# A list scheduler that counts loads of ScalarE's function tables, with another table of due times

## The chip, the cores and the metric

One Trainium2 chip; the kernel runs on one of its cores. The metric is the device time of one execution in microseconds (us). Engines are called as in the profile: PE (TensorE matmul, PEld its weight loads), DVE (VectorE), ACT (ScalarE), POOL (GpSimd), SP (the engine that only issues DMAs).

## What is computed

One layer of a hybrid block on 512 positions of width 1024, in float32:

```python
h = rmsnorm(x) ; proj = h @ w_in                 # gb, gc, v | u, ug | q | three gates
y_a = (gb * conv3(gc * v)) @ w_a_out             # short gated convolution
y_b = silu(layernorm(conv31(u * sigmoid(ug)))) @ w_b_out
y_c = attention(q, rmsnorm(mem) @ w_kv) @ w_att_out    # 4 heads, 256 memory tokens
m = sigmoid(g0) * y_a + sigmoid(g1) * y_b + sigmoid(g2) * y_c
x = x + m @ w_o
up = conv3(rmsnorm(x) @ w_up) ; x = x + (silu(gate half) * up half) @ w_down   # width 2816
return rmsnorm(x)
```

## The kernel before

**Arithmetic.** Each float32 operand of a product is split in two fp32r parts, high and low, and three products are added: high by high, low by high, high by low. ACT makes the high part by a cast (weights "wh", line 481; activations "fh", line 1357), DVE the low part by a subtraction ("wl", line 485; "fl", line 1361). A weight tile thus goes from its DMA over ACT and DVE to PE.

**Quads.** The large products are computed by a Strassen-like scheme: seven products for a 2 by 2 block, a *quad* (names glu, q, gate, cv, bb, mq, up). The sums of weights that the scheme needs are made by DMAs of POOL that add to what has landed ("s3", "s5", "s6", "s7", line 606). The products' banks are read out by ACT ("r1", "r5", "r6", "r4") and DVE ("r2", "r7", "r3"): r6 reads the bank of product 6 (line 701), which product 7 overwrites; r4 is the last read of ACT (line 709).

**Stages in order of time.** Keys and values of the memory (line 915 and the products K and V); the projection quads; between them the attention (exponentials, line 1068) and the 31 taps of branch B ("tp" on ACT, line 1224, two per job; sums on DVE, line 1231); from about 438 us LayerNorm statistics, the gates' sigmoids (line 1481, two or four per row), the swish of branch B (line 1322), whose casts (line 1357) feed the last projection quads "mq" (branch B's output product, 510 to 552 us); the product by w_o (lines 432 to 434), in seven parts a, b, f, c, d, e, g, with additions to x on DVE (line 1719); the second RMSNorm: square (line 1726), root (1732), reciprocal (1736), scaling (1737), transpose on PE (1745); then the up quads, the FFN's convolution and silu gate, the down products and the last norm.

**The order of work.** PE's order is written by hand. All other instructions are *jobs* of a list scheduler (`Jobs.run`), which replays the program with estimated costs and issues, step by step, the job that can start first; of several, the one that is due first. A job's due time comes from `latest_starts`: the planned start of the product that needs it, less the costs on the way, plus a number for its kind from the table LATER. A kind in AHEAD also isn't started earlier than so many us before it is due. The order found is frozen, so that it is the order of each engine's queue. These two lines of `run` choose:

```python
rank = (start, due[key])
if best is None or rank < best[0]:
```

The scheduler of before knows no function tables: where a job on ACT uses a function that isn't in the table loaded last, the compiler puts a load (ACT_TABLE_LOAD) ahead of it. Sigmoid, silu (swish), exponential and square root lie in different tables; copies, casts and squares need none.

Of the kernel before, what the change touches and what calls it, by code (L numbers as in the profile page):

```python
# [61 lines left out]
SHARE = 0.39  # L62
SEEN = {"PE": 0.2, "ACT": 0.14, "DVE": 0.12}
# [7 lines left out]
    "ACT fh y t4": 45, "ACT pth": -72, "ACT r1 mq": -5, "ACT r4 cv": 36, "ACT r4 gate": 12.12,  # L71
    "ACT r5 gate": 28.56, "ACT sigmoid": 32.54, "ACT tp 1": -18.64, "ACT tp 2": 21.22,
# [5 lines left out]
    "DVE tap 2": -72, "DVE tap 3": 173, "DVE top": 49, "DVE vl": 125, "DVE weigh": 125,  # L78
# [9 lines left out]
    "ACT fh y t7": 5, "ACT r4 gate": 5, "ACT r5 gate": 40, "ACT sigmoid": 80, "ACT tp 1": 150,  # L88
# [25 lines left out]
class Jobs:  # L114
# [109 lines left out]
    def run(self, log=None):  # L224
# [4 lines left out]
        for key, j in self.jobs.items():  # L229
            waits[key] = len(set(j[3]))  # L230
            if j[0] == "PE":
                pe.append(key)
            elif not waits[key]:
                ready.setdefault(j[0], {})[key] = 0.0
            for name in j[6]:
                self.left[name][0] += 1
        free = {e: 0.0 for e in ["PE"] + sorted({j[0] for j in self.jobs.values()} - {"PE"})}
        pe.reverse()
        n = len(self.jobs)
        while n:  # L240
            best = None
            for e in free:
# [74 lines left out]
def hybrid_block_kernel(  # L317
# [19 lines left out]
    nc = tc.nc  # L337
# [340 lines left out]
    def quad_reads(q, first, second, ring, after=(), all_but_4=False):  # L678
# [16 lines left out]
        job(("r1", q), "ACT", actv(512), read1, [(q, 1)] + list(after),  # L695
# [3 lines left out]
        job(("r5", q), "ACT", actv(512), read5, [(q, 5)] + list(after),  # L699
            take=[(second, ring)], use=[bank("b")])  # L700
        job(("r6", q), "ACT", actv(512), lambda: nc.scalar.copy(f()[:, :, hi_t], view("a")),
# [7 lines left out]
        job(("r4", q), "ACT", actv(512), lambda: nc.scalar.activation(  # L709
# [1071 lines left out]
    for t in range(NT):  # L1781
# [8 lines left out]
        for i in range(2):  # L1790
            bank, r = ("bank", "tr", t, i), t // 2
            if (i, r) != (0, 1):
                job(("rh", t, i), "ACT", actv(512), lambda t=t, i=i: row_high(t, i), [("tr", t)],
# [5 lines left out]
            job(("rb", t, i), "ACT", actv(512), lambda t=t, i=i: row_block(t, i), [("tr", t)],  # L1799
# [508 lines left out]
```

## Time and profile before

| what | value |
|---|---|
| median of 3 runs (range) | 930.26 us (929.43 to 931.14) |
| the profiled execution | 929.14 us |
| its span, first to last instruction | 927.4 us |
| mean granted TensorE clock | 0.997 |
| busy: PE, DVE, ACT, POOL | 98%, 91%, 74%, 15% of the span |
| loads of function tables on ACT in the order | 13 |

How to read it: a row of the timeline has the start, the duration, the engine, the line of the program, the operation, what it writes and reads by the program's names, and in brackets how long the engine sat idle before it and what ended that. A row with x2 stands for two instructions in a row. The table by stretches has the busy time and the count of each engine in each stretch. All of it is of one execution.

### The profile page before, as it was taken

How to read it: one execution, taken by the hardware profiler on the slowest of the kernel's cores; microseconds unless marked ns; L12 is line 12 of the kernel's file. 1: busy time of each engine (PE TensorE's matmuls, PEld its weight loads, DVE VectorE, ACT ScalarE, POOL GpSimd, SP SyncE). 2: the span in 40 equal slices, each digit the busy share in tenths (PEclk: the TensorE clock that was granted, in tenths of full speed). 3: DMA queues.
4: the chain of work that ended last, by engine and by line, in shares of the span. 5: the costliest groups of instructions: out<-in, count | busy, mean ns of one | idle time of the engine just before them, and what ended most of it. 6: DMA issues, size and time to landing. Idle time of an engine off the chain costs nothing.

```text
span 927.4 us, 17128 instructions
## 1 busy us (share of the span) xinstructions
PE 912.5 (98%) x6821; PEld 861.6 (93%) x6821; DVE 847.8 (91%) x973; ACT 685.8 (74%) x935; POOL 137.0 (15%) x165
## 2 busy tenths in 40 slices
PE   9999999999999999999999999999999999999996
PEld 8999999999989999999899897799999999988885
DVE  6998999999979999999886999897999889999986
ACT  7567988889978876878766982786766667765665
POOL 0121111101011111110111111111221111002300
PEclk9999999999999999999999999999999999999998
DMA  9999678845588888888858899899999885689952
GB/s 355 389 243 220 143 183 199 189 114 114 155 181 232 199 191 203 215 198 207 198 130 219 195 250 327 213 231 305 275 248 235 193 168 125 176 310 310 252 110 91
DMA packets 55952, 196.91 MB, mean 212 GB/s; under 512 B 6336, under 2 KB 6464, under 8 KB 55872
## 3 DMA queue, kind: packets, MB, share of 16 engines
q0 software_dynamic: 22608, 81.54, 48.6%
q1 hardware_dynamic: 32544, 113.23, 33.6%
q8 instruction: 53, 0.87, 0.4%
q10 hardware_dynamic: 720, 1.06, 0.3%
q14 instruction: 27, 0.22, 0.1%
HBM read 191.60 MB, written 4.19 MB: 211 GB/s over the span
## 4 chain that ended last, share of the span: by engine, by line
PE 88%; ACT 5%; DVE 3%; DMA 2%; issue 1%; SPq 0%; ACTq 0%; DVEq 0%
PE bank L658 57%; PE bank L432 6%; PE bank L434 6%; PE bank L433 6%; PE bank L1456 3%; PE bank L1457 3%; PE bank L1458 3%; PE bank L915 2%; ACT whi L481 1%; DVE wlo L485 1%; DMA wf<-in_w_up 1%; PE bank L1690 1%; DMA wf<-in_w_v 1%; ACT acc L1322 1%; PE ss L788 0%
## 5 line engine op out<-in xcount | busy, mean ns | idle before, releaser
L481 ACT CAST whi<-wf 128x1024 fp32r<-128x1024 f32 x202 | 210.7, 1045 | 90.0 <-PE bank L658 36.5
L485 DVE TENSOR_TENSOR wlo<-wf,whi 128x1024 fp32r<-128x1024 f32 (+1 forms) x196 | 236.3, 1213 | 21.7 <-ACT whi L481 21.5
L1224 ACT ACTIVATE tp<-u,pk 128x510 f32<-128x510 f32 (+22 forms) x184 | 119.2, 706 | 4.5 <-DVE acc L1231 2.1
L1231 DVE TENSOR_TENSOR acc<-acc,tp 128x988 f32<-128x988 f32 (+22 forms) x92 | 109.3, 1189 | 8.8 <-ACT tp L1224 7.3
L606 POOL DMA_DIRECT2D wf<-in_w_in x48 | 42.4, 899 | 233.4 <-DVE wlo L485 165.5
L658 PE MATMUL bank<-fb10h,whi 128*128 128x256 f32 x248 | 69.0, 278 | 1.6 <-ACT g L709 1.2
L658 PE MATMUL bank<-ft4h,whi 128*128 128x256 f32 (+1 forms) x249 | 68.7, 276 | 0.9 <-DVE y L438 0.9
L658 PE MATMUL bank<-fb10l,whi 128*128 128x256 f32 x248 | 68.6, 277 | 0.6 <-DVE fb10l L1361 0.6
L658 PE MATMUL bank<-ft6h,whi 128*128 128x256 f32 (+1 forms) x250 | 68.8, 277 | 0.2 <-ACT gt L686 0.2
L658 PE MATMUL bank<-ft5l,whi 128*128 128x256 f32 x248 | 68.8, 277 | 0.0
L658 PE MATMUL bank<-ft6l,whi 128*128 128x256 f32 x248 | 68.7, 277 | 0.0
L658 PE MATMUL bank<-ft5h,whi 128*128 128x256 f32 (+1 forms) x251 | 68.7, 276 | 0.0
L658 PE MATMUL bank<-fb11h,wlo 128*128 128x256 f32 x248 | 68.6, 277 | 0.1
L658 PE MATMUL bank<-fb11h,whi 128*128 128x256 f32 x248 | 68.7, 277 | 0.0
L658 PE MATMUL bank<-fb00h,whi 128*128 128x256 f32 (+1 forms) x250 | 68.7, 276 | 0.0
L658 PE MATMUL bank<-ft6h,wlo 128*128 128x256 f32 x248 | 68.6, 277 | 0.0
L658 PE MATMUL bank<-fb00l,whi 128*128 128x256 f32 x248 | 68.6, 277 | 0.0
L658 PE MATMUL bank<-ft4l,whi 128*128 128x256 f32 x248 | 68.6, 276 | 0.0
L658 PE MATMUL bank<-ft5h,wlo 128*128 128x256 f32 x248 | 68.5, 276 | 0.0
L658 PE MATMUL bank<-ft7h,whi 128*128 128x256 f32 x248 | 68.5, 276 | 0.0
L658 PE MATMUL bank<-ft7l,whi 128*128 128x256 f32 x248 | 68.5, 276 | 0.0
L658 PE MATMUL bank<-ft7h,wlo 128*128 128x256 f32 x248 | 68.5, 276 | 0.0
(406 smaller groups left out, 3167.7 us busy)
## 6 DMA issues: line engine op xcount, KB each, us to landing
wf<-in_w_in SPq DMA_DIRECT2D x52, 512.0 KB, 5.4
wf<-in_w_in POOLq DMA_DIRECT2D x48, 512.0 KB, 6.1
wf<-in_w_up POOLq DMA_DIRECT2D x31, 512.0 KB, 7.3
wf<-in_w_up SPq DMA_DIRECT2D x29, 512.0 KB, 7.9
wf<-in_w_down SPq DMA_DIRECT2D x15, 512.0 KB, 4.4
wf<-in_w_att_out SPq DMA_DIRECT2D x8, 512.0 KB, 3.6
wf<-in_w_a_out SPq DMA_DIRECT2D x8, 512.0 KB, 3.6
wf<-in_w_b_out SPq DMA_DIRECT2D x8, 512.0 KB, 6.2
```

Of the source, the lines that this page charges most:

```text
L432: nc.tensor.matmul(ps, s_hi, w_hi, start=start, stop=False, skip_group_check=again)
L433: nc.tensor.matmul(ps, s_hi, w_lo, start=False, stop=False, skip_group_check=again)
L434: nc.tensor.matmul(ps, s_lo, w_hi, start=False, stop=stop, skip_group_check=again)
L481: nc.scalar.copy(parts[0], src())
L485: nc.vector.tensor_tensor(lo, src(), hi.bitcast(F32), op=ALU.subtract)
L606: nc.gpsimd.dma_start(out=tiles[key], in_=block(w, col[c], k), accum_op=ALU.add)
L658: nc.tensor.matmul(ps[:, c, part], w[:, k, at], a[k][:, part], start=first and n == 0 and part.start == 0, stop=k == 3 and n == 2, skip_gr ...
L1224: nc.scalar.activation(two(("tp", p, s))[:, j, s:], two(("u", p))[:, j, : SEQ - s], AF.Copy, scale=weight(j),)
L1231: nc.vector.tensor_tensor(a, a, two(("tp", p, s))[:, :, s:], op=ALU.add)
L1456: nc.tensor.matmul(ps, w_hi[:, i, at], hi, start=first, stop=False)
L1457: nc.tensor.matmul(ps, w_hi[:, i, at], lo, start=False, stop=False)
L1458: nc.tensor.matmul(ps, w_lo[:, i, at], hi, start=False, stop=last)
```

## The change

No instruction of arithmetic and no DMA is added or removed, and PE's order stays. Four things change in the planning.

1. The scheduler keeps the table that is loaded. A job that needs another one, and isn't due within 3 us, is ranked as if it started 1.28 us later; a job that changes the table costs 1.28 us more in the plan.
2. The planned cost of ACT's reads of a bank in the quads and behind the second norm falls from (n + 224)/1200 - 0.08 to (n + 68)/1200 us, for 512 columns from 0.53 to 0.48.
3. The planned costs of a quad's product and of a whole w_o product fall by under 1.2%.
4. The tables LATER and AHEAD are replaced by longer ones, with an entry for most kinds of jobs and shifts of up to 1500 us.

```diff
+TABLES = {
+    "ACT sg": "sigmoid", "ACT sigmoid": "sigmoid", "ACT swish": "silu", "ACT silu": "silu",
+    "ACT exp": "exp", "ACT m root": "sqrt", "ACT x root": "sqrt", "ACT v root": "sqrt",
+    "ACT xroot": "sqrt", "ACT rt": "sqrt",
+}
+TABLE_LOAD, TABLE_WAIT = 1.28, 3.0
...
 LATER = {
-    "ACT fh y t4": 45, "ACT pth": -72, "ACT r1 mq": -5, "ACT r4 cv": 36, "ACT r4 gate": 12.12,
+    "ACT c3": -619, "ACT exp": -81, "ACT fh h b00": -432.7, "ACT fh h b10": -180,
...
+        table = None
...
-                        rank = (start, due[key])
+                        late = TABLES.get(self.kind(key), table) != table
+                        late = late and due[key] + lag - start > TABLE_WAIT
+                        rank = (start + TABLE_LOAD if late else start, due[key])
                         if best is None or rank < best[0]:
-                            best = (rank, e, key, got)
+                            best = (rank, e, key, got, start)
...
-            (start, _), e, key, got = best
+            _, e, key, got, start = best
             _, cost, fn, after, latency, _, names = self.jobs[key]
+            if TABLES.get(self.kind(key), table) != table:
+                table, cost = TABLES[self.kind(key)], cost + TABLE_LOAD
...
+    def from_bank(n):
+        return (n + 68) / 1200.0
...
-    MM, MM_HALF, MM_QUAD = 0.2268, 0.12, 0.1142
-    MM_WHOLE = 0.87
+    MM, MM_HALF, MM_QUAD = 0.2268, 0.12, 0.1135
+    MM_WHOLE = 0.86
...
-        job(("r6", q), "ACT", actv(512), lambda: nc.scalar.copy(f()[:, :, hi_t], view("a")),
+        job(("r6", q), "ACT", from_bank(512), lambda: nc.scalar.copy(f()[:, :, hi_t], view("a")),
```

About 460 of 738 jobs on ACT stand at another place than before (by up to 35), 612 of 899 on DVE (by up to 72), 110 of 220 on SP (by up to 6) and 59 of 157 on POOL (by up to 6). Line numbers of the changed kernel are higher by 102 behind the tables. ACT has 11 loads of tables: between the root of the LayerNorm (row 416 in both) and the end of the mq quads there were five, for sigmoid, silu, sigmoid, silu, sigmoid, and are three, sigmoid, silu, sigmoid. One pair of sigmoids moves ahead of the LayerNorm's root, another behind the fifth load. At the read r6 of the last cv quad, the largest difference of that part, eleven jobs of taps and a weight cast now stand ahead of it that stood behind, and two casts and one bias product behind it that stood ahead.

Three places, in rows of the order (line, operation, tiles with their numbers, shape). First ACT in the mq stage, where the swish of the last channel blocks (acc_3230 and acc_3978; acc_3197 and acc_3917 in the changed kernel) is cast for the product with fb10. Before:

```order
L481 CAST whi_6112<-wf_5878 128x1024
L1481 ACT_TABLE_LOAD
L1481 ACTIVATE g_5783<-g_5783,pk 128x512 x2
L686 COPY y_6145<-bank_6082 128x2x256
L1357 CAST ft6h_6149<-acc_1093 128x512
L481 CAST whi_6153<-wf_5923 128x1024
L1357 CAST ft4h_6156<-acc_3230 128x512
L1322 ACT_TABLE_LOAD
L1322 ACTIVATE acc_3978<-acc_3978,pk 128x512 x2
L686 COPY y_6191<-bank_6120 128x2x256
L1357 CAST fb10h_6078<-acc_3978 128x512
```

And the changed kernel:

```order
L583 CAST whi_6103<-wf_5958 128x1024
L1459 CAST fb10h_6109<-acc_3197 128x512
L1459 CAST fb11h_6113<-acc_3197 128x512
L1459 CAST ft7h_6116<-acc_1093 128x512
L1424 ACTIVATE acc_3917<-acc_3917,pk 128x512 x2
L788 COPY y_6150<-bank_6078 128x2x256
L1459 CAST fb10h_6109<-acc_3917 128x512
L583 CAST whi_6154<-wf_5888 128x1024
```

The two loads and the pair of sigmoids between the last two swish jobs are gone; the sigmoids of g_5783 stand some 20 rows further down, behind those of g_5924.

Second, ACT behind w_o, the norm of the first two row tiles of x. Before:

```order
L481 CAST whi_6799<-wo_6664 128x1024
L1726 ACTIVATE xnorm_6812,cols<-x_833_6520 128x1024
L1726 ACTIVATE xnorm_6815,cols<-x_841_6564 128x1024
L1732 ACT_TABLE_LOAD
L1732 ACTIVATE cols<-cols,eps 128x1 x2
L481 CAST whi_6833<-wf_6690 128x1024
```

And the changed kernel:

```order
L583 CAST whi_6786<-wo_6695 128x1024
L1828 ACTIVATE xnorm_6800,cols<-x_839_6560 128x1024
L1834 ACT_TABLE_LOAD
L1834 ACTIVATE cols<-cols,eps 128x1
L583 CAST whi_6818<-wo_6634 128x1024
L1828 ACTIVATE xnorm_6831,cols<-x_842_6599 128x1024
L583 CAST whi_6840<-wf_6778 128x1024
```

The first root stands ahead of the second square; the second root comes behind both. On DVE the low part of whi_6818 takes the place of the second scaling, between the first scaling and the next two additions to x.

Third, SP at the start of the program, where mem are half tiles of the memory and wf weights. Before:

```order
L850 DMA wf_98<-in_w_v 128x512 x2
L511 DMA wf_119<-in_w_v 128x1024
L741 DMA mem_99<-in_mem_t 128x512 x2
L511 DMA wf_151<-in_w_kv 128x1024
L511 DMA wf_168<-in_w_kv 128x1024
```

And the changed kernel:

```order
L952 DMA wf_98<-in_w_v 128x512 x2
L843 DMA mem_99<-in_mem_t 128x512 x2
L613 DMA wf_128<-in_w_v 128x1024
L613 DMA wf_151<-in_w_kv 128x1024
L613 DMA wf_172<-in_w_kv 128x1024
```

The weight V(0,1) is loaded behind the two half tiles instead of ahead of them, and ACT's casts of it and of the half tiles change places in the same way.

More of the change, by code (lines that the diff above doesn't have):

```diff
@@ new lines @@
+    "ACT sr": -334, "ACT swish": 252, "ACT tap 1": -214.4, "ACT tap 2": -191, "ACT tap 3": -547.5,
[8 rows of a table added]
+    "ACT wn wo 0": -774.4, "ACT x root": 121, "ACT xroot": -5.5, "ACT xsq": -18, "ACT xsquare": 15,
[8 rows of a table added]
+    "DVE low": 39.7, "DVE m scale": -418, "DVE mgl a": 159, "DVE mgl b": 325.5, "DVE mgl d": 11,
+    "DVE mgl e": 647.4, "DVE mgl g": -351, "DVE ml": 15, "DVE ms c": -142, "DVE ms d": -3.5,
+    "DVE ms e": 328, "DVE msum": -143, "DVE mu fold": -89, "DVE mu low": -614, "DVE mu sum": -395,
+    "DVE ol": -34, "DVE pn": -193, "DVE ptl": -147, "DVE ql": -1183.6, "DVE r2 bb": -176.3,
[5 rows of a table added]
@@ L85 @@
+    "DVE rd f": -4, "DVE rd g": 51.4, "DVE sc": -297.1, "DVE sum": -988.2, "DVE tap 1": -30,
+    "DVE tap 2": 25.4, "DVE tap 3": 51.2, "DVE top": -7.9, "DVE tot1": -8, "DVE tot2": -44,
+    "DVE um": -1259, "DVE var fold": 4.7, "DVE var sum": -23.3, "DVE vl": 737, "DVE weigh": 547,
[18 rows of a table added]
+    "POOL s7 up": -142, "POOL wadd e": -277, "POOL wadd x": 2.1, "POOL wadd y": -65,
[6 rows of a table added]
 }
 AHEAD = {
-    "ACT fh y t7": 5, "ACT r4 gate": 5, "ACT r5 gate": 40, "ACT sigmoid": 80, "ACT tp 1": 150,
[4 rows of a table removed]
+    "ACT fh h b00": 80, "ACT fh h b11": 150, "ACT fh h t4": 40, "ACT fh h t6": 40,
@@ new lines @@
+    "ACT rt": 10, "ACT sq": 150, "ACT tap 1": 10, "ACT tap 2": 20, "ACT tap 3": 150,
[4 rows of a table added]
+    "ACT wn merge 0": 5, "ACT xroot": 40, "ACT xsquare": 150, "ACT zh c": 150, "ACT zh g": 5,
+    "DVE CV": 80, "DVE c3": 80, "DVE centre": 150, "DVE ends": 150, "DVE fl h b00": 150,
[5 rows of a table added]
+    "DVE ol": 150, "DVE pn": 20, "DVE ptl": 40, "DVE ql": 5, "DVE r2 glu": 20, "DVE r2 q": 5,
+    "DVE r2 up": 40, "DVE r3 gate": 150, "DVE r3 glu": 80, "DVE r3 q": 10, "DVE r7 bb": 20,
+    "DVE r7 gate": 20, "DVE r7 glu": 2, "DVE r7 mq": 10, "DVE r7 up": 40, "DVE rd a": 40,
@@ L93 @@
+    "DVE rd c": 2, "DVE rd d": 150, "DVE rd f": 40, "DVE sum": 150, "DVE top": 5, "DVE tot1": 20,
[5 rows of a table added]
+    "DVE xnorm": 150, "DVE xsum": 5, "DVE y t4": 10, "DVE y t5": 150, "DVE y t6": 10,
[5 rows of a table added]
+    "POOL wadd x": 150, "POOL wadd y": 80, "POOL wl merge 0": 10, "POOL wl merge 2": 20,
[4 rows of a table added]
 }
@@ L693, in add @@
             nc.vector.tensor_tensor(t, t, b, op=ALU.add)
-        job(("r1", q), "ACT", actv(512), read1, [(q, 1)] + list(after),
+        job(("r1", q), "ACT", from_bank(512), read1, [(q, 1)] + list(after),
             take=[(first, ring)], use=[bank("a")])
@@ L698, in quad_reads @@
             [(q, 2), ("r1", q)], use=[bank("c"), first])
[L699 removed]
+        job(("r5", q), "ACT", from_bank(512), read5, [(q, 5)] + list(after),
             take=[(second, ring)], use=[bank("b")])
[L701 removed]
+        job(("r6", q), "ACT", from_bank(512), lambda: nc.scalar.copy(f()[:, :, hi_t], view("a")),
             [(q, 6), ("r1", q)], use=[bank("a"), first])
@@ L708, in quad_reads @@
             return
-        job(("r4", q), "ACT", actv(512), lambda: nc.scalar.activation(
+        job(("r4", q), "ACT", from_bank(512), lambda: nc.scalar.activation(
             s()[:, :, lo_t], view("a"), AF.Copy, scale=-1.0), [(q, 4), ("r5", q)],
```

15 lines of the change are left out of this document (11 added, 4 removed), and 92 rows, old and new, of tables (AHEAD, LATER).

## The prediction

> **What bounds the kernel now.** I read the page first: its span and the busy times.
>
> ```profile
> span 927.4 us, 17128 instructions
> PE 912.5 (98%) x6821; PEld 861.6 (93%) x6821; DVE 847.8 (91%) x973; ACT 685.8 (74%) x935; POOL 137.0 (15%) x165
> ```
>
> TensorE is busy for 912.5 of 927.4 us, and its products are the same after the change, in the same order. So only the 14.9 us in which it isn't busy can change. The table by stretches (columns: stretch, its length, then busy time and count of PE, PEld, DVE, ACT, POOL, then the granted clock, the DMA share and GB/s) says where they lie.
>
> ```profile
> 0.00:50.00 50.00, 48.17 (x320) 44.58 (x321) 40.24 (x57) 33.34 (x45) 3.51 (x11) 1.00 0.99 363
> 300.00:400.00 100.00, 100.00 (x885) 100.00 (x884) 98.15 (x105) 77.11 (x106) 18.51 (x22) 1.00 0.86 201
> 500.00:600.00 100.00, 95.30 (x612) 82.97 (x611) 89.90 (x111) 75.02 (x99) 16.51 (x19) 1.00 0.92 243
> 600.00:700.00 100.00, 99.70 (x870) 99.11 (x870) 91.21 (x105) 71.82 (x94) 19.11 (x22) 1.00 1.01 263
> 900.00:928.00 28.00, 19.36 (x117) 17.14 (x115) 19.48 (x34) 15.82 (x30) 0.00 (x0) 0.90 0.20 75
> ```
>
> 1.8 us lie at the start, 4.7 between 500 and 600, 0.3 between 600 and 700, and 8.6 behind 900, nearly all of them the tail after the last product. The granted clock is 1.00 wherever products run. The 4.7 us are four waits in the last quads of the input projection (the quads "mq") and two behind w_o, as the timeline shows (start, duration, engine, line, operation, in brackets the idle time and what ended it):
>
> ```profile
> 526.60 0.39 PE L658 MATMUL bank<-fb10h,whi 128*128 128x256 f32 x1 [0.45 <-ACT fb10h L1357]
> 527.54 0.39 PE L658 MATMUL bank<-fb10l,whi 128*128 128x256 f32 x1 [0.55 <-DVE fb10l L1361]
> 531.00 0.38 PE L658 MATMUL bank<-fb10h,whi 128*128 128x256 f32 x1 [1.19 <-ACT g L709]
> 545.79 0.38 PE L658 MATMUL bank<-ft4h,whi 128*128 128x256 f32 x1 [0.91 <-DVE y L438]
> 592.34 1.06 PE L1745 MATMUL bank<-ident,xnorm 128*128 128x128 f32 x8 [0.77 <-DVE cols L1736]
> 594.24 0.50 PE L432 MATMUL bank<-whi,mgh 128*128 128x512 f32 x1 [0.84 <-DVE x L1719]
> ```
>
> The bracket is less than what is lost, since the matmul before is counted busy while it drains. From start to start, a 128x256 product follows the one before after 0.11 us (885 in the 100 us of 300:400), and the last start ahead of each wait is:
>
> ```profile
> 525.88 0.28 PE L658 MATMUL bank<-fb10h,wlo 128*128 128x256 f32 x1
> 529.53 0.28 PE L658 MATMUL bank<-fb10h,wlo 128*128 128x256 f32 x1
> 544.61 0.28 PE L658 MATMUL bank<-ft7h,wlo 128*128 128x256 f32 x1
> 591.18 0.39 PE L434 MATMUL bank<-whi,mgl 128*128 128x512 f32 x1
> ```
>
> So the first place loses 526.60 - 525.88 - 0.11 = 0.61, the second 527.54 - 526.60 - 0.11 = 0.83, the third 531.00 - 529.53 - 0.11 = 1.36 and the fourth 545.79 - 544.61 - 0.11 = 1.07: 3.9 us in all. What ends the first three is ScalarE (the second by way of VectorE), which has no room there: 9.97 of 10 us in the first row below. The second row has 40 products of w_o in 10 us, 0.25 each; with it the two waits behind w_o are 592.34 - 591.18 - 0.25 = 0.91 and 594.24 - 592.34 - 0.88 (eight transposes at 0.11) = 1.02: 1.9 us.
>
> ```profile
> 520.00:530.00 10.00, 8.81 (x73) 8.21 (x71) 8.40 (x12) 9.97 (x16) 1.75 (x2) 1.00 1.01 231
> 560.00:570.00 10.00, 10.00 (x40) 7.32 (x40) 9.97 (x12) 3.05 (x3) 0.34 (x1) 1.00 1.03 355
> ```
>
> **The change part by part.** *The list of tables.* It takes two loads out of this stretch (the order rows of the section on the change) and moves sigmoids out of it. A load costs 1.28 us, a sigmoid pair 1.34, and the load below begins 0.02 us after the cast ahead of it ends (530.83 + 1.05), and the next activation follows it within 0.02:
>
> ```profile
> 525.93 0.62 ACT L1357 CAST fb10h<-acc 128x512 fp32r<-128x512 f32 x1
> 530.35 0.60 ACT L709 ACTIVATE g<-bank 128x512 f32<-128x512 f32 x1
> 530.83 1.05 ACT L481 CAST whi<-wf 128x1024 fp32r<-128x1024 f32 x1
> 531.90 1.28 ACT L1481 ACT_TABLE_LOAD   x1
> 533.20 1.34 ACT L1481 ACTIVATE g<-g,pk 128x512 f32<-128x512 f32 x2
> 539.28 0.28 PE L658 MATMUL bank<-ft7h,whi 128*128 128x256 f32 x1
> ```
>
> On ACT a row runs into the next by about 0.1 (530.35 to 530.83 for a read of 0.60), so a weight cast takes 0.95 and a bank read or a 512-wide cast 0.5. Counted from the sigmoid load that both orders have (row 421), the cast of 525.93 has 7.2 us less ahead of it: two loads (2.6), two sigmoid pairs (2.7), one weight cast (0.95), one bank read (0.5), and one 512-wide cast fewer on balance (0.5). It can stand at about 519 if nothing it needs is late, and at 521 or 522 if it waits for the bank read ahead of it; TensorE wants it at 526. The bank read of 530.35 has 4.7 us less ahead: two loads, two pairs and a weight cast less (6.2), three 512-wide casts more (1.5). It comes at 525.7; TensorE, 1.44 earlier by the first two waits, wants it at 528.2. So 1.9 us are left over, and the first three waits go. The fourth is VectorE's (line 438, behind reads that ACT now does earlier); I take it as gone too. But two sigmoid pairs and a load now stand ahead of the reads of the second half: from 525.7 ACT has the read, three weight casts, the load, two pairs and two more weight casts (9.2 with the read) before the read that must be done when product 7 of mq 0 begins. That product began at 539.28, which the first three waits make 536.5; the read would be done at 535.5. The 1.0 left over is about one weight cast that has to wait for its DMA. Bounds: all 3.9 back, or 2 of it lost again; I take 0.8 lost: **-3.1**.
>
> The Trainium skill speaks of this price. Its page "ScalarE: Activation LUTs", section "What ACT_TABLE_LOAD costs", puts a switch at about 1283 ns of load and some 1380 ns of draining, 2.66 us in all. The trace has the load at that length and no drain around it, so the measurement decides; by that price the two loads would free 5.3 us instead of 2.6, the 0.8 would not be lost, and the sum would be 0.8 better.
>
> *The norm behind w_o.* The order before has both squares, the load, both roots, both scalings. The changed one has the first square, the load, the first root and the first scaling, and everything of the second row tile behind them.
>
> ```profile
> 586.88 1.05 ACT L1726 ACTIVATE xnorm<-x 128x1024 f32<-128x1024 f32 x1
> 587.93 1.05 ACT L1726 ACTIVATE xnorm<-x 128x1024 f32<-128x1024 f32 x1
> 590.38 0.48 ACT L1732 ACTIVATE cols<-cols,eps 128x1 f32<-128x1 f32 x2
> 590.91 1.28 DVE L1737 SCALAR_TENSOR_TENSOR xnorm<-x,cols,gffn 128x1024 f32<-128x1024 f32 x1
> 593.50 1.28 DVE L1719 TENSOR_TENSOR x<-x,bank 128x512 f32<-128x512 f32 x2
> ```
>
> One square (1.05) and one root (0.24) leave the way of the first scaling, 1.3 us against a wait of 0.91. VectorE's additions at 593.50 stood behind the second scaling (1.28); a weight's low part of nearly the same length stands there now, so they come earlier by the same 1.3, against 1.02. Both waits go, with 0.3 to spare, if nothing upstream holds the first square (586.88, behind the cast of a weight): **-1.9** (bounds -1.9 and 0).
>
> *The start.* SP now issues two memory half tiles (512 KB together) ahead of the load of V(0,1), and ACT casts them first.
>
> ```profile
> 9.78 1.05 ACT L481 CAST whi<-wf 128x1024 fp32r<-128x1024 f32 x1 [0.66 <-DMA wf<-in_w_v]
> 10.86 1.23 DVE L485 TENSOR_TENSOR wlo<-wf,whi 128x1024 fp32r<-128x1024 f32 x1 [1.02 <-ACT whi L481]
> 12.25 0.39 PE L433 MATMUL bank<-wlo,mh 128*128 128x512 f32 x1
> PE bank L915 <- DVE wlo L485: 0.5, 1, 0.5
> ```
>
> The cast at 9.78 waits for the landing and the low part is done at 12.09, 0.16 before its product. 512 KB at the 363 GB/s of 0 to 50 take 1.4 us, so the product comes some 1.2 us late. The wait of the next weight (0.5 in the table of waits, 0.6 by pitch) then goes, as its own load stands where it stood: +0.6 to +1.2, I take **+0.9**.
>
> *All else.* The planner's new costs of a bank read and of a product are no instructions; they act through the order alone. Some 450 ACT and 600 VectorE jobs change places in stretches where TensorE waits for nothing; what hides them is the room between a job and its product. Small waits may come where it is thin; I put one in for the dozen quads, the size of the small ones here (0.45 above): **+0.4** (bounds 0 and the third rival). The 0.3 us at 650 stay: the load order of the up weights there only changes by a few places. The tail stays at 8 us: the last chain of output additions has the same instructions.
>
> Sum: -3.1 - 1.9 + 0.9 + 0.4 = **-3.7**. The profiled execution took 929.14 us (span 927.4 and 1.7 around it), 1.1 under the median of 930.26. It would become 925.4, and the median **926.5**.
>
> **The rivals.** *All of it comes back.* With no losses in the second half of mq and no small waits, the sum is -3.9 - 1.9 + 0.6 = -5.2: 925.1. For it: 1.0 and 1.9 us of room above; against it, DVE at 98% in 300:400.
>
> *The DMAs of w_o keep their time.* ACT waits there 2.16 us for an accumulated weight, and casts it and splits it (1.05 and 1.23) just ahead of the product of w_o that uses it:
>
> ```profile
> 585.92 1.05 ACT L481 CAST whi<-wo 128x1024 fp32r<-128x1024 f32 x1 [2.16 <-DMA wo<-in_w_o]
> 569.66 0.86 POOL L1603 DMA_DIRECT2D wo<-in_w_o  x1 [12.32 <-DVE wlo L485]
> ```
>
> If it lands when it does now, all that was won or lost before it is evened out by a wait there, and only the -1.9 behind it is left: 928.4. Against it: POOL issues them only because VectorE's low part at 569.66 holds the queue for 12.32 us, and that part is now several places earlier on VectorE. For it: the DMA share of 1.03. The Trainium skill, "DMA: Bandwidth & Descriptors", section "Issuing engines are not separate DMA queues", says that transfers of all issuing engines share the same 16 DMA engines; this full share agrees, and by it an earlier issue alone would win less than it moves.
>
> *The bank reads of 290 to 430 come late* (the side of a loss). Each quad's sixth product is read by ACT (line 701) before the seventh may overwrite the bank.
>
> ```profile
>   PE bank L658: 7.8, 6
> 289.28 0.59 ACT L701 COPY C<-bank 128x512 f32<-128x512 f32 x1 [0.80 <-PE bank L658]
> 291.80 0.28 PE L658 MATMUL bank<-ft7h,whi 128*128 128x256 f32 x1
> 406.13 1.31 ACT L1224 ACTIVATE tp<-u,pk 128x501 f32<-128x501 f32 x2
> ```
>
> ACT sits idle before six of the eight reads here, 1.3 us each (first row, time and count), and 291.80 - 289.87 = 1.9 pass until the product: it may come 3.2 later than now. Ahead of the read of the last conv quad now stand eleven pairs of tap products (1.31 each) and a weight cast (1.05) that stood behind it, less two casts (2.1) and a bias product (0.7): 12.7 us of work. If the idle time before it can't take that up, the read is up to 9.5 late, if half is taken up 3.2. It is slower by over 0.2% once more than 5.6 is lost; I price it at 7.5: 934.0. Against it: ACT is idle for 23 of 100 us in 300:400, 15 of them ahead of this read, and a tap can run as soon as its input is there.
>
> That the change doesn't do what it says is excluded by the order: 11 loads on ACT where there were 13.
>
> **How the numbers follow.** Forecast -3.7: 0.47; all of it: 0.20; DMAs of w_o: 0.14; late bank reads: 0.19. A measurement of this kernel can tell about 0.2% from no change, 1.9 us: below 928.4 is faster. The forecast, the first rival and 0.04 of the second are (0.71); the other 0.10 of the second, whose time is the border itself, and the mildest 0.02 of the third are the same (0.12); the rest of the third is slower (0.17). The range takes in the first rival with 2 us for what is mis-sized in it, the second, and the near part of the third, up to where the read is 5.5 late: 922.9 to 932.0.
>
> **What would show it.** Right: ACT with two loads fewer between 500 and 535, and no wait at the products on fb10 nor on the bank read after them; the transposes after w_o without a wait on the reciprocal; the first V product about 1 us late. Wrong: waits of TensorE for ACT's bank reads between 290 and 430, or on w_o's low parts at 580, or the fourth mq wait still there, as VectorE is full between 540 and 570.

## The result, and the profile after

| | before | changed |
|---|---|---|
| median of 20 executions | 929.79 us | 931.57 us |
| lowest and highest | 928.93, 935.74 | 926.63, 938.77 |
| the profiled execution, its span | 929.14, 927.4 | 926.63, 924.8 |

The ratio of the means is 1.0007 with a 95% interval of 0.9986 to 1.0028: no change that can be told. The two rows below it say more. The lowest executions of the changed kernel are 2.3 us below the lowest of before, and its profile is the lowest of its 20: 926.63, where the sum of the prediction gave 925.4 for the profile and 926.5 for the median. But 11 of its 20 executions lie over 3 us above the lowest, against 2 of 20 before, and the median lies among those. So there are two questions: what the profile gained and lost, and what the profile doesn't show.

The page of the changed kernel, its span and busy times:

```profile
span 924.8 us, 17087 instructions
PE 911.2 (99%) x6821; PEld 860.7 (93%) x6821; DVE 849.1 (92%) x973; ACT 681.4 (74%) x933; POOL 137.2 (15%) x165
```

ACT has two instructions fewer (933 for 935), the two loads. TensorE isn't busy for 13.6 us instead of 14.9. Where these are has moved, as the table by stretches of the changed kernel shows (columns as above: stretch, length, busy time and count of PE, PEld, DVE, ACT, POOL, then clock, DMA share, GB/s):

```profile
0.00:50.00 50.00, 47.88 (x321) 44.17 (x322) 39.87 (x56) 34.65 (x46) 3.51 (x11) 1.00 0.99 369
400.00:500.00 100.00, 99.31 (x709) 92.63 (x709) 85.44 (x88) 67.98 (x89) 12.65 (x15) 1.00 0.81 190
500.00:600.00 100.00, 100.00 (x662) 88.76 (x661) 94.17 (x118) 76.10 (x103) 18.23 (x21) 1.00 0.96 256
600.00:700.00 100.00, 97.13 (x850) 96.36 (x849) 87.91 (x98) 68.08 (x88) 18.61 (x22) 1.00 1.01 262
900.00:925.00 25.00, 16.97 (x106) 15.18 (x104) 17.63 (x33) 14.94 (x29) 0.00 (x0) 0.93 0.22 84
```

500 to 600 went from 95.30 to 100.00 of 100 us. 600 to 700 went from 99.70 to 97.13, and 0.69 us came in between 400 and 500. TensorE's table of waits names what it waits for now (total, times, longest):

```profile
PE bank L760 <- ACT gt L788: 1.1, 1, 1.1
PE bank L760 <- DVE uu L540: 0.9, 1, 0.9
PE bank L535 <- DVE wlo L587: 0.8, 1, 0.8
PE bank L760 <- ACT g L803: 0.7, 1, 0.7
PE bank L760 <- DVE ft5l L676: 0.6, 1, 0.6
```

None of the six waits that the prediction showed is there: no fb10, no y, no cols, no x, and no bank read on line 811 (709 before). "gt", "uu" and "ft5l" (lines 788, 540, 676) are tiles of the up quads, "g" is a bank read of a gate quad. In the timeline of TensorE, the predicted places first, then the new waits, each with the last start ahead of it:

```profile
405.84 0.28 PE L760 MATMUL bank<-ft5h,wlo 128*128 128x256 f32 x1
406.81 0.39 PE L760 MATMUL bank<-ft7h,whi 128*128 128x256 f32 x1 [0.69 <-ACT g L803]
...
526.21 0.28 PE L760 MATMUL bank<-fb10h,whi 128*128 128x256 f32 x1
...
587.99 1.03 PE L1847 MATMUL bank<-ident,xnorm 128*128 128x128 f32 x8
588.78 0.48 PE L534 MATMUL bank<-whi,mgh 128*128 128x512 f32 x1
...
610.71 0.28 PE L760 MATMUL bank<-ft5h,whi 128*128 128x256 f32 x1
611.63 0.39 PE L760 MATMUL bank<-ft5l,whi 128*128 128x256 f32 x1 [0.65 <-DVE ft5l L676]
638.76 0.28 PE L760 MATMUL bank<-ft5h,wlo 128*128 128x256 f32 x1
639.93 0.36 PE L760 MATMUL bank<-ft4h,whi 128*128 128x256 f32 x1 [0.90 <-DVE uu L540]
645.35 0.28 PE L760 MATMUL bank<-fb11h,wlo 128*128 128x256 f32 x1
646.74 0.39 PE L760 MATMUL bank<-ft6h,whi 128*128 128x256 f32 x1 [1.11 <-ACT gt L788]
```

The fb10 products and the transposes (line 1847) have no bracket: nothing was waited for. The transposes begin at 587.99, 4.35 us earlier than before. By the reckoning of the prediction (start to start, less 0.11) the new waits cost 0.86 at 406, 0.81 at 611, 1.06 at 639 and 1.28 at 645. Added up the same way over all products, the waits by stretch are:

```
stretch      before  changed   difference
0-50           2.5     2.7       +0.1
400-500        0.1     1.0       +0.9
500-550        4.3     0.1       -4.2
550-600        2.5     0.6       -2.0
600-650        1.0     4.1       +3.1
behind 800     0.3     0.7       +0.4
```

Of 6.2 us won between 500 and 600, 3.1 are lost again in the 50 us behind.

ACT's timeline of the changed kernel shows what was late at 406, a late weight in the up quads, and the cast and the bank read on which the first term was built:

```profile
404.28 1.06 ACT L1434 CAST yah<-ya 128x1024 fp32r<-128x1024 f32 x1 [2.10 <-DVE ya L1534]
405.24 1.04 ACT L583 CAST whi<-wf 128x1024 fp32r<-128x1024 f32 x1
406.19 0.57 ACT L803 COPY g<-bank 128x512 f32<-128x512 f32 x1
...
519.82 0.62 ACT L1459 CAST fb10h<-acc 128x512 fp32r<-128x512 f32 x1
...
526.89 0.61 ACT L811 ACTIVATE g<-bank 128x512 f32<-128x512 f32 x1
...
632.37 1.05 ACT L583 CAST whi<-wf 128x1024 fp32r<-128x1024 f32 x1 [3.62 <-DMA wf<-in_w_up]
```

At 404 ACT sits 2.10 us before a cast whose input VectorE has not finished, and the bank read of 406.19 is queued behind it and a weight cast. At 632 it sits 3.62 us before the cast of an accumulated weight; before the change its longest wait for a weight between 600 and 650 was 1.45. Whether this weight makes the waits of the up quads is tried below.

### The profile page after: what moved, and what is told of

Same layout as the page of the kernel before. It is cut to its first block, busy times and chain, and to the rows that moved or that the text cites. A ratio compares the mean times of both kernels' runs of the same rounds, so it can differ in the third digit from the quotient of the medians.

```text
span 924.8 us, 17087 instructions
## 1 busy us (share of the span) xinstructions
PE 911.2 (99%) x6821; PEld 860.7 (93%) x6821; DVE 849.1 (92%) x973; ACT 681.4 (74%) x933; POOL 137.2 (15%) x165
## 3 DMA queue, kind: packets, MB, share of 16 engines
q10 hardware_dynamic: 720, 1.06, 0.3%
## 4 chain that ended last, share of the span: by engine, by line
PE 84%; DVE 6%; DMA 5%; issue 2%; ACT 1%; SPq 0%; ACTq 0%; DVEq 0%; POOLq 0%
PE bank L760 52%; PE bank L535 6%; PE bank L536 6%; PE bank L534 6%; PE bank L1558 3%; PE bank L1559 3%; PE bank L1560 3%; DMA wf<-in_w_in 3%; DVE wlo L587 2%; PE bank L1017 2%; DMA wf<-in_w_up 2%; DVE upc L1514 1%; PE bank L1792 1%; DVE gtc L1514 1%; ACT whi L583 1%
## 5 line engine op out<-in xcount | busy, mean ns | idle before, releaser
L587 DVE TENSOR_TENSOR wlo<-wf,whi 128x1024 fp32r<-128x1024 f32 x198 | 238.3, 1211 | 26.9 <-ACT whi L583 26.6
L1333 DVE TENSOR_TENSOR acc<-acc,tp 128x1022 f32<-128x1022 f32 (+22 forms) x92 | 109.1, 1188 | 4.1 <-ACT tp L1326 2.4
L708 POOL DMA_DIRECT2D wf<-in_w_in x50 | 44.4, 895 | 242.7 <-DVE wlo L587 163.0
L760 PE MATMUL bank<-ft4h,wlo 128*128 128x256 f32 x248 | 68.5, 276 | 0.0
L760 PE MATMUL bank<-fb11l,whi 128*128 128x256 f32 x248 | 68.5, 276 | 0.0
```

What stands on the lines that cost most here:

```text
L587: nc.vector.tensor_tensor(lo, src(), hi.bitcast(F32), op=ALU.subtract)
L708: nc.gpsimd.dma_start(out=tiles[key], in_=block(w, col[c], k), accum_op=ALU.add)
L760: nc.tensor.matmul(ps[:, c, part], w[:, k, at], a[k][:, part], start=first and n == 0 and part.start == 0, stop=k == 3 and n == 2, skip_gr ...
L1333: nc.vector.tensor_tensor(a, a, two(("tp", p, s))[:, :, s:], op=ALU.add)
```

## The experiments

An order can be cut and joined. In all kernels below except rule_alone and due_alone, the scheduler no longer chooses: it issues a list written out beforehand, in again that of the change, in most others that of before up to one product and that of the change from there, or the other way round. The instructions are the same in each but for the loads of tables, of which ACT has 11 in each kernel and 13 in up_as_after. The edit, once for all:

```diff
+ORDER = [('mem tile', 0), ('ldm', 0, 0),
...
+]
...
-            for e in free:
+            for at, key in enumerate(todo):
+                e = self.jobs[key][0]
+                if e in blocked:
+                    continue
...
+                        best = todo.pop(at)
```

Results, with the number of executions over 3 us above the kernel's lowest as a measure of scatter. Each row was compared with the kernel before on the same chip (there 929.76 to 930.83):

| kernel | n | median | lowest, highest | over 3 above lowest | ratio, 95% |
|---|---|---|---|---|---|
| again | 12 | 932.51 | 927.31, 939.62 | 8 | 1.0007 (0.9978 to 1.0036) |
| up_as_before | 12 | 928.62 | 926.12, 932.81 | 6 | 0.9974 (0.9950 to 0.9998) |
| up_as_after | 12 | 932.69 | 931.94, 938.80 | 3 | 1.0033 (1.0008 to 1.0058) |
| mid_as_after | 12 | 929.90 | 928.60, 936.18 | 3 | 0.9985 (0.9958 to 1.0012) |
| mq_to_up_only | 5 | 924.33 | 922.79, 924.41 | 0 | 0.9933 (0.9907 to 0.9959) |
| mq_to_up_again | 7 | 924.25 | 923.29, 930.41 | 2 | 0.9919 (0.9884 to 0.9955) |
| start_as_before | 12 | 927.82 | 926.34, 934.94 | 4 | 0.9987 (0.9966 to 1.0008) |
| start_alone | 9 | 924.28 | 923.55, 929.90 | 1 | 0.9919 (0.9889 to 0.9949) |
| up_loads_as_before | 10 | 929.18 | 926.36, 933.99 | 4 | 0.9977 (0.9950 to 1.0003) |
| up_act_dve_as_before | 10 | 931.98 | 926.31, 938.90 | 9 | 1.0002 (0.9970 to 1.0033) |
| rule_alone | 4 | 954.28 | 952.86, 954.92 | 0 | 1.0258 (1.0227 to 1.0288) |
| due_alone | 4 | 950.21 | 947.72, 953.06 | 1 | 1.0217 (1.0178 to 1.0256) |

### The change by stretches: four kernels

**again**: the changed kernel once more.

> The changed kernel once more, its order written out as a list of jobs. All theories: the same scatter as in its 20 runs (926.6 to 938.8 us), so a median near 931 with runs more than 3 us apart. If the profiled execution is one of the long ones, its waits of TensorE show where the excess lies: theory U (up stage, 600 to 700 us, weights that land late) expects waits of over 5 us in all there; theory W (w_o) at 545 to 590; theory R (bank reads) at 290 to 430.

The median is 2.7 above that of before, with the same wide scatter. Its profile is again the lowest execution (927.31) and has the same new waits (1.15 at 406, 0.81, 0.68 and 1.09 in the up quads).

**up_as_before**:

```diff
-order of the change throughout
+order of the change up to product 1 of up 0, order before from there
```

> The changed kernel's order up to the first product of the up stage, the order of before from there on. Theory U (the loss and the scatter come from the up stage): 924 to 926 us, runs within 2 us of each other, no wait of over 0.5 us behind 600. Theory W or R: scatter and median stay, 929 to 933.

The median falls by 3.9 us against again, the lowest only by 1.2 (by 0.5 against the lowest of the 20 above), and half of the executions still scatter upwards. So the up quads' order costs some 1 us in the lowest, and isn't the only origin of the scatter.

**up_as_after**:

```diff
-order before throughout
+order before up to product 1 of up 0, order of the change from there
```

> The order of before up to the first product of the up stage, the changed one from there on. Theory U: it scatters over 5 us or more, and lies above before, at 933 to 937 us, with the waits between 600 and 700. Theory W or R: 930 to 933, runs within 2 us.

The reverse: 2.9 us over the kernel before in the median, 3.3 in the lowest, and no more scatter than before has. The up part alone is a loss; and it isn't the earlier arrival of TensorE, as here TensorE arrives no earlier (in the profile 1.4 us later, since behind its waits at w_o the granted clock was 0.51 from 594.5 to 598 us). It waits for the same three tiles as in the changed kernel:

```profile
619.09 0.39 PE L1213 MATMUL bank<-ft5l,whi 128*128 128x256 f32 x1 [0.46 <-DVE ft5l L1129]
646.83 0.36 PE L1213 MATMUL bank<-ft4h,whi 128*128 128x256 f32 x1 [0.37 <-DVE uu L993]
653.64 0.38 PE L1213 MATMUL bank<-ft6h,whi 128*128 128x256 f32 x1 [0.92 <-ACT gt L1241]
```

**mid_as_after**:

```diff
-order before throughout
+order before up to merge 0 (439 us), order of the change up to product 1 of up 0, order before from there
```

> The changed order only from the first product of the branch outputs at 439 us to the up stage; before and behind it the order of before. All of the 3.9 us in the mq stage and 1.9 us behind w_o should come back: theories U and R: 923.5 to 925 us with runs within 2 us; theory W: 927 to 931 with scatter. R also expects it 0.9 us or more below the second kernel of this set.

The waits of mq and behind w_o are gone and the median doesn't move. The table of waits of this kernel has the reason in its first row, and it is the experiment's own:

```profile
PE bank L2013 <- DMA wlo<-in_w_a_out: 3.7, 1, 3.7
```

Where the two orders are joined, at 455 us, a weight's buffer is late, which costs 3.9 us from start to start. Behind it the granted clock was 0.50, products of 512 columns came every 0.43 us instead of every 0.23, and 2.6 us more were lost:

```profile
458.00:464.00 6.00, 5.09 (x12) 4.02 (x13) 5.58 (x7) 5.88 (x9) 0.87 (x1) 0.50 1.06 252
```

If its lowest execution, of which there is no profile, lost these 6.5 us too, it would be 922.1 without them: an estimate. Besides, the profiled execution took 935.74 and has 852 products where 885 belong between 700 and 800: this was the first sight of the second pace, told below.

### The gain by itself, and the second pace

**mq_to_up_only**: the same with the joint put where no buffer is short.

```diff
-order before up to merge 0 (439 us), order of the change up to product 1 of up 0, order before from there
+order before up to product 7 of gate 1,0 (477 us), order of the change up to product 1 of up 0, order before from there
```

> The order before up to 477 us (product 7 of quad gate 1,0) and from the up quads on; between them the changed order, with no seam of two orders beside a weight that is short. Theory P (pace): a stretch of 128x256 products without a break runs at 113.3 or at 117.8 ns a product, is set to one of them where it begins, and the scatter of the changed kernel comes from its front (45 to 440 us). Then this kernel has the executions of the kernel before, 5.8 us lower: most at 922.8 to 925.2, about one in four some 6 us above, median 924. Its profile has no waits at the products on fb10, at the bank reads behind them, at the fourth wait of mq or behind w_o, and none at 406. Rival S (the scatter is in what the change did between 477 and 605): executions spread over 923 to 935 without two groups, median 926 to 929. Rival N (the 5.8 us are given back): 928 to 930.

All five executions lie between 922.8 and 924.4. Theory P had 922.8 to 925.2. This is the version that beats both kernels, the one before by 0.7% with an interval clear of 1.

**mq_to_up_again**: no edit.

> The kernel of mq_to_up_only once more. Theory P: executions at 922.8 to 925.2 as before, and now and then (in the kernel before about one in four, on this chip perhaps fewer) one some 6 us above; median 924 to 925. Rival S (the five executions so far were lucky, the front of the kernel scatters whatever its order): median above 926.

Five executions at 923.3 to 924.9, two at 929.5 and 930.4; and the profiled one is one of these two (929.53), beside 923.66 for the profile of mq_to_up_only. So one kernel was caught in both of its times. TensorE's rows in the profile at 923.66: two waits in the up quads, two products that are 42 apart, and 50 us of the table by stretches:

```profile
641.31 0.38 PE L1213 MATMUL bank<-fb11h,wlo 128*128 128x256 f32 x1 [0.34 <-DVE wlo L1040]
644.31 0.39 PE L1213 MATMUL bank<-ft6h,whi 128*128 128x256 f32 x1 [0.22 <-ACT gt L1241]
...
699.74 0.28 PE L1213 MATMUL bank<-fb11h,wlo 128*128 128x256 f32 x1
704.50 0.28 PE L1213 MATMUL bank<-ft5h,wlo 128*128 128x256 f32 x1
```

```profile
700.00:750.00 50.00, 50.00 (x444) 50.00 (x443) 44.93 (x53) 33.58 (x42) 7.82 (x9) 1.00 0.90 194
```

The same in the profile at 929.53, which has no bracket between 640 and 646:

```profile
699.81 0.28 PE L1213 MATMUL bank<-fb10h,whi 128*128 128x256 f32 x1
704.75 0.28 PE L1213 MATMUL bank<-ft6h,whi 128*128 128x256 f32 x1
```

```profile
700.00:750.00 50.00, 50.00 (x427) 50.00 (x426) 43.03 (x51) 32.83 (x41) 8.62 (x10) 1.00 0.88 192
```

4.76 us for 42 products is 0.1133 each, 4.94 is 0.1176: 4% longer, with TensorE busy throughout, waiting for nothing, and a granted clock of 1.00 in both rows. 17 products in 50 us are 1.9 us, and the pace holds from 605 to 805 us, behind which both profiles run alike. The 1,366 products between 644 and 805 make 6.1 us at 4.5 ns each; the two times differ by 5.9.

### Where the scatter starts

**start_as_before**:

```diff
-order of the change throughout
+order before up to product 1 of glu 0 (45 us), order of the change from there
```

> The changed kernel with the order before up to the first product of the dozen quads (45 us): V(0,1) loaded and cast ahead of the memory half tiles. Theory P1 (the start sets the pace of the stretch 45 to 172, and that is the scatter): most executions within 2 us of 926 (the lowest of the changed kernel, 926.6, less the 0.9 of the start), at most one in four some 5 to 6 us above, median 926.5. Rival P2 (the break at 406, or another behind 45, makes the scatter): spread as in the changed kernel, 925.5 to 935, more than a third above 929, median 929 to 931.

927.82 lies between the two theories, and a third of the executions is above 929.3: it doesn't decide.

**start_alone**: mq_to_up_only with the start of the change, in SP's order:

```diff
-ld V(0,1)
 ldm 1,0
 ldm 1,1
+ld V(0,1)
```

and the same on ACT and VectorE.

> mq_to_up_only with only the start of the change: the two memory half tiles are loaded, cast and split ahead of V(0,1), 3 places on SP, 4 on ACT, 3 on VectorE. Theory P1 (the start sets the pace of the stretch 45 to 172, and so the scatter): 0.9 longer in the lowest executions (923.7), and executions spread over 923.7 to 930 with more than a third above 927; a profile with 117.8 ns a product between 45 and 172 where it falls on such an execution. Rival Q (the start only costs its 0.9): all but one or two executions at 923.7 to 926, median 925.2.

Eight of nine executions at 923.6 to 924.9, the median that of mq_to_up_only. Theory P1 falls, and so does the price of 0.9 in rival Q. At the start of this profile TensorE waits once for a weight, 0.50 us, where the profile of before has a wait of 0.47 for the next weight:

```profile
12.81 0.50 PE L987 MATMUL bank<-wlo,mh 128*128 128x512 f32 x1 [0.50 <-DVE wlo L1039]
```

So the start alone doesn't bring the scatter. Neither does what comes behind 439: mid_as_after and mq_to_up have the changed order there up to the up quads, up_as_after has it from there on. Taking all kernels together: with the changed order between 45 and 439, 42 of 76 executions lie over 3 us above the kernel's lowest; with the order before there, 34 of 144 (25 of 99 of the kernel before among them). The share of the kernel before differs from set to set of runs (1 of 17 to 12 of 27), but in each of the four sets the changed order in this stretch has the larger one (11 of 20 against 2 of 20, 14 of 24 against 16 of 59, 4 of 12 against 1 of 22, 13 of 20 against 15 of 43). What in these 394 us does it was not tried apart, and no kernel has the changed order there alone, so it may need another part with it.

### The two halves of the change

**rule_alone**: the scheduler's rule and the new planned costs, with the due times of before.

```diff
+                        late = TABLES.get(self.kind(key), table) != table
+                        late = late and due[key] + lag - start > TABLE_WAIT
+                        rank = (start + TABLE_LOAD if late else start, due[key])
...
 LATER = {
     "ACT fh y t4": 45, "ACT pth": -72, "ACT r1 mq": -5, "ACT r4 cv": 36, "ACT r4 gate": 12.12,
```

> The counting of table loads and the new costs of bank reads and products, with the due times of the kernel before; 11 loads on ACT, as in the changed kernel. Theory L (the two loads are the gain): the waits of the quads mq are gone, 925 to 928. Rival F (rule and due times are fitted to each other): the jobs change places elsewhere and weights or reads come late there; slower than before by 5 us or more, 935 to 955, with new waits of TensorE for VectorE's low parts or for bank reads.

**due_alone**: the new due times without the rule.

```diff
-                        late = late and due[key] + lag - start > TABLE_WAIT
+                        late = False
...
-            if TABLES.get(self.kind(key), table) != table:
-                table, cost = TABLES[self.kind(key)], cost + TABLE_LOAD
```

> The changed due times without the counting of table loads; also 11 loads on ACT. Theory D (the due times do the work, the rule adds nothing that they don't give): 926 to 932, as the changed kernel. Rival F (fitted to each other): slower by 5 us or more than the kernel before, 935 to 955, with waits in the up quads and in w_o that the changed kernel doesn't have.

Each has the 11 loads, and each is 20 to 25 us slower. The largest waits of TensorE with the rule alone:

```profile
PE bank L672 <- ACT whi L495: 6.2, 3, 3.8
PE bank L672 <- ACT ft5h L584: 5.2, 1, 5.2
PE bank L672 <- DVE wlo L499: 4.6, 4, 1.9
```

and with the due times alone:

```profile
PE bank L533 <- DMA whol<-in_w_o: 4.8, 1, 4.8
PE bank L758 <- DVE ft5l L674: 3.3, 1, 3.3
PE bank L758 <- ACT B L801: 2.2, 1, 2.2
PE bank L758 <- ACT gt L786: 2.1, 1, 2.1
```

Most of these waits (at 55 and 245 us with the rule alone, at 332, 565 and 629 with the due times alone) are for weights, forms and bank reads with no load of a table within 10 us; the one on gt, at 668, stands 4 us behind a load. Behind most of the long ones the granted clock was 0.50 to 0.52 for 3 to 7 us, so that the wait of 4.8 for w_o's weight cost 8.0 in all. The four waits of before in the mq quads are gone with the rule alone, and all but 0.4 us of them with the due times alone. The rival F holds: the numbers of a due-time table belong to the rule that they were made with, and what either half loses elsewhere is far more than the two loads bring.

### The up quads: loads or engines

**up_loads_as_before** and **up_act_dve_as_before**:

```diff
-order of the change throughout
+DMA issues (in the second kernel: ACT's and VectorE's jobs) from product 1 of up 0 on in the order before
```

> The changed kernel with the DMA issues of SP and POOL from the first up product on in the order before (the accumulation s5 of up 2 ahead of s3 of up 1 again). Theory G (the loads' order makes the 3.5 us of waits of the up quads): the 3.62 us of ACT for that weight at 632 shrink to under 2, and the waits at 639 and 645 (2.3 us) go; those at 611 may stay. Rival H (the order of ACT and VectorE makes them): the waits at 611, 639 and 645 stay, 2.5 us or more.

> The changed kernel with the jobs of ACT and VectorE from the first up product on in the order before, the DMA issues as in the change. Theory H (ACT and VectorE's order makes the up quads' waits): waits of the up quads no more than 1.5 us, as in up_as_before without the one at 411. Rival G (the loads' order): the waits at 639 and 645 stay, 2 us or more, the cast of the late weight still holding ACT.

TensorE's waits in the up quads with the loads of before:

```profile
PE bank L1209 <- ACT gt L1237: 0.9, 1, 0.9
PE bank L1209 <- DVE uu L989: 0.8, 1, 0.8
PE bank L1209 <- DVE ft5l L1125: 0.6, 1, 0.6
```

and with ACT's and VectorE's order of before:

```profile
PE bank L1210 <- DVE ft6l L1126: 0.7, 1, 0.7
PE bank L1210 <- DVE wlo L1037: 0.5, 1, 0.5
PE bank L1210 <- DVE uu L990: 0.2, 1, 0.2
```

Theory G falls: with the loads back all three waits are still there, 3.2 us from start to start with the small ones, and ACT still waits 2.22 us for a weight at 633. With the engines' order back the one on gt is gone and that on uu is 0.2, but a new one on ft6l has come, and 2.6 us are left, where H expected 1.5 at most. So H isn't borne out either.

The same two products, one of w_o at 600.27 us in the profile before and one near the end at 906.12, measure the loss in the profiles of the changed kernel and of the joined orders, apart from those with a long stretch at the second pace between the two:

| kernel | ACT and VectorE from the up quads on | DMA issues from there on | TensorE ahead at the first product | time to the second, over the 305.8 of before |
|---|---|---|---|---|
| mq_to_up_only, start_alone | before | before | 6.8, 6.7 | 1.1, 1.1 |
| up_as_before | before | before | -0.1 | 1.9 |
| up_loads_as_before | change | before | 5.8 | 3.0 |
| up_act_dve_as_before | before | change | 5.8 | 2.9 |
| changed, again, start_as_before | change | change | 5.5, 5.0, 5.3 | 3.1, 3.3, 2.6 |
| up_as_after | change | change | -1.4 | 3.1 |

The changed order of the up stage loses 3.1 us whether TensorE comes 5.5 us earlier or 1.4 us later, and the old order loses less with a lead of 6.8. So the loss comes from the order of that stage, not from the lead. Either half of it alone leaves nearly all of the loss; which jobs make it isn't settled.

## Why the prediction was right and wrong

*The list of tables: -3.1.* Right in its mechanism, 1 us too small. The four waits are gone, and the 0.8 "lost again" was not. The cast of the last fb10 came at 519.82 where the prediction had "about 519", or 521 to 522; the bank read at 526.89 where it had 525.7, for a product that wants it at 528.2. mq_to_up_only shows that the gain comes from the order between 477 and the up quads, as nothing else is changed in it. That it is the two loads and the moved sigmoids within that order is supported, not shown: rule_alone and due_alone, in other orders with the same 11 loads, are without these four waits too (but for 0.4 us of the last in due_alone), and up_as_after, with 13, has them; but rule_alone has 5 us of other waits between 538 and 557, for the high and low parts of weights.

*The norm behind w_o: -1.9.* As predicted, in every kernel that has this part. The rival that the DMAs of w_o keep their time falls: the transposes came 4.35 us earlier, all that had been won.

*The start: +0.9.* The right sign, the wrong size. The product with the low part of the first V weight came 0.65 us later than before (12.90 for 12.25), where 1.4 us of DMA less a slack of 0.16 had been taken for 1.2; the wait of 0.63 at 15 went, as said. Together the waits of that stretch are 0.1 longer, and start_alone shows no difference in the time.

*All else: +0.4.* This step failed. It measured +4.4: 0.9 at 406, 3.1 in the up quads, 0.4 behind 800. The prediction put its 0.4 in "the dozen quads" and said of the up quads that "the 0.3 us at 650 stay: the load order of the up weights there only changes by a few places". That argument looked at the loads alone. ACT and VectorE have another order there too, and with either half put back 2.9 to 3.0 us of loss remain, with both back 1.1 to 1.9. The nearest rival, that TensorE now comes too early for its feeders, falls: in up_as_after it comes 1.4 us later than before and loses the same 3.1 at the same three tiles. So the new order of the stage brings forms and bank reads late, although TensorE lost only 1.0 us to waits between 600 and 650 before. The prediction worked out job by job what ACT does in mq; the up quads, where VectorE was busy for 91.21 of 100 us in the row 600:700, got no such reckoning. The tail stayed near 8 us, as said; the 8.6 given for it count the 0.6 between the end of the span and 928.

*The rival of the bank reads* came true at one read of eight, for 0.9 us instead of the 5.6 at which it decides: ACT's idle time took up the taps, as argued. The late input at 404.28 is VectorE's, which the rival didn't name.

*From the profile to the median.* The waits add to -1.7 and the span fell by 2.6 (0.4 of the rest are 90 products, at 16 and at 617 us, that ran at the second pace in the profile of before and at the first in this one). So the profile came at 926.63, 1.2 over its forecast. The median did not follow. The step behind it, "its products are the same after the change ... So only the 14.9 us in which it isn't busy can change", is the one that failed: the products have two paces, a long stretch at the second costs 4.7 to 6 us, and with the changed order between 45 and 439 the executions over 3 us above the lowest are more than twice as frequent. That an order changes the scatter is shown by the count above. That the scatter is this pace is shown for the times that a profile caught (931.19 of up_as_before, 935.74 of mid_as_after, 929.53 of mq_to_up_again, each 5 to 7 above the lowest of its kernel, each with one long stretch at the second pace). The first of these has the changed order up to the up quads, and lost 4.7 us between 45 and 168 against the profile of again. For the changed kernel itself no high execution was profiled; there it is an inference. One long stretch can't be all of it: in the set of 35 executions the kernel before has two groups, 928.6 to 931.0 and 934.7 to 936.3, but the changed kernel's executions lie at all distances between 926.6 and 938.8. A lower granted clock isn't it: the mean clock of the 20 is 0.996 to 0.999, and 0.997 in the longest.

That the median of 931.57 lies between the stated 922.9 and 932.0 is luck. The upper end was there for late bank reads, and these cost 0.9 us; what brought the median there was the pace, or more generally the scatter, which the prediction didn't have.

## What to carry to other kernels

A planner's table that is tuned for the whole program can be cut by stretches: an order that gains 5.5 us in one stage and loses in others is worth taking over for that stage alone, with the joint put where no buffer is short. A stage whose order changes has to be reckoned anew even where nothing waits now: the up quads lost 1.0 us to waits before and some 3 us more by their new order, with TensorE early or late. And a profile of one execution, above all of the lowest, can't stand for a median: look at the list of times first, and count the products in equal stretches.

## What the hardware showed that was not expected

TensorE repeated the same weight load and 128x256 product every 113.3 ns or every 117.8 ns, with the granted clock at 1.00 in both. In the 14 profiles of this study the three long stretches with few breaks (45 to 167, 287 to 438 and 645 to 805 us, of 900 to 1,360 products each) were compared. 38 of 42 ran at 113.3, four at 117.8: 45 to 175 in up_as_before, 298 to 433 in due_alone, 607 to 811 in mid_as_after and 605 to 805 in mq_to_up_again. The row of up_as_before, and below it the same stretch of mq_to_up_only:

```profile
100.00:150.00 50.00, 50.00 (x427) 50.00 (x426) 48.31 (x51) 41.96 (x59) 8.63 (x10) 1.00 0.88 183
```

```profile
100.00:150.00 50.00, 50.00 (x444) 50.00 (x443) 49.83 (x53) 43.34 (x61) 7.80 (x9) 1.00 0.80 175
```

A long stretch has its pace from its first products on and keeps it across quads and tiles. Where it changes there is nearly always a break: a wait, products of another width, or a single product that starts 0.05 to 0.1 us late (0.05 in due_alone at 298 us). In mq_to_up_only 95 products from 605 on ran at the second pace, and a wait of 0.16 us at 616 ended it; in mq_to_up_again the product there was only 0.05 late, and the pace stayed for 200 us. A break doesn't always change it: in due_alone a wait of 2.3 us at 332 left it as it was. What chooses it wasn't found.

The Trainium skill, "TensorE: Matmul & The Clock Gate", section "Back-to-back issue gap", says that in a stream of such pairs the spacing is set by the weight load and the product together, and gives one sustained spacing each for 128 and 512 columns. For 256 columns these runs show two, at one granted clock.
